# A gate unit moved from the v stage into the scan, a wider parameter tile, and an earlier load of the first initial states

## The chip, the cores and the metric

The kernel runs on one core of a Trainium2 chip. The metric is device microseconds of one execution. A core has TensorE (PE, matmuls; PEld is its weight load), VectorE (DVE), ScalarE (ACT) and GpSimd (POOL), each with its own instruction stream in a fixed order; SyncE (SP) issues the DMAs of this kernel. [...]

## The reference

One step of a hybrid backbone, one layer, with D = 1024, on 1024 latent tokens and 128 context tokens that share the weights:

```python
# sub-layer 1, the token mixers on one normalised and modulated input h
z, xbc, dt_raw, u, v, ga, gb = split(h @ w_in)
x, B, C = split(silu(conv3(xbc)))            # x 2048 wide, B and C 512 wide
y_f, hf = ssd_chunked(x * dt_f, dt_f * A_f, B, C, h0_f)     # chunks of 128, 32 heads of 64
y_b, hb = the same backwards
y_ssd = rmsnorm((y_f + y_b + d * x) * silu(z))
y_sgu = u * (sgu_w @ layernorm(v) + sgu_b)   # per 128-token chunk and 128-channel group
x1 = x0 + gate1 * rmsnorm((sigmoid(ga) * (y_ssd @ w_bs) + sigmoid(gb) * (y_sgu @ w_bu)) @ w_out)
# sub-layer 2, the ConvFFN
up = depthwise3x3(h2 @ w_up);  a, val = split(up)           # 2 x 2816 channels
x2 = x1 + gate2 * rmsnorm((gelu(a) * val) @ w_down)
```

In the chunked scan a state of 128 x 64 per head runs from chunk to chunk; the latent scans start from states given as inputs (h0), the context's scans from zero. Outputs are the tokens and the context's final states.

## The kernel before

All 1152 tokens are kept channel by channel in three blocks of 384 tokens. Every float32 product is made of three matmuls on halves of the operands, high x high, high x low, low x high (`gemm_cm`, L293). The inputs are resident as hh and hl. The weights stream through `Weights` (L58 on): pieces of 128 x 512 (256 KB) are loaded by SP into three raw buffers wr (L70), then split by ACT (a cast into wh, L82) and DVE (a subtraction into wl, L83). There are four buffers of wh and wl; for six of the eight pieces of a v half the room is a pair of larger tiles, vwh and vwl. `W.advance(n)` splits n more pieces and issues the loads that lie three ahead; `W.take(n)` hands out pieces.

A **unit** (`inproj`, L423) makes 128 output channels from two pieces: for each of three token blocks 24 matmuls into a PSUM bank "gps" out of three (`gbank`), an advance by one piece in the second and third block, and a sink that consumes the bank. The **gate unit** (`gate_unit`, L615) has as its sink a copy by ACT into an SBUF tile gt (L618) and a store of gt by SP to a scratch in DRAM (L619), from where the gate is read again much later. Where gt lies and how many buffers it has is set by `gtp`: one buffer in the scan's pool ssdA, three in a pool opened after the scan.

The **scan** works on 16 pairs of heads in 17 rounds. A round interleaves the steps of a pair (transposes ptX, decays R and EP on ACT, yd, yo and state matmuls pst and pstc, H products on DVE) with filler units (x, z, B, C, gate) that keep PE busy. `load_R` and `load_E` bring the decays of a pair from DRAM, `load_H` (L661) its initial states. For the first pair they are issued after the pool ssdA opens, behind the first x unit: R and EP for three segments, then H. The end of a pair (DVE L605, ACT L606 and L608, store L609) multiplies by the gate z and stores to yssd_scr.

After the scan its pools are closed and others opened at the same place. Then comes the **v stage**: for each of two halves of 512 channels, a gate unit, then nine v tiles (`v_tile`): 24 matmuls of 512 columns (L906 to L908) into a bank "pv" from the same three as the gate's, a copy by ACT into vtok (L910), statistics on DVE. The dot products of a modulation run on DVE beside it, and the u units follow.

In the **ConvFFN** the up-projection goes to tiles U; the convolution takes eight of nine taps on DVE (L1200), each acc = U * w + acc with the weight from a parameter tile fpar.

The order within an engine is made by a list scheduler when the program is built: it takes instructions in the order of the code with priorities, so an instruction moved in the code moves others too.

Of the kernel before, what the change touches and what calls it, by code (L numbers as in the profile page):

```python
# [4 lines left out]
F32 = mybir.dt.float32  # L5
# [25 lines left out]
MT_DT, MT_U, MT_B, MT_C, MT_X, MT_Z, MT_GA, MT_GB = 0, 1, 9, 13, 17, 33, 49, 57  # L31
# [75 lines left out]
def body(tc, A, O):  # L107
# [4 lines left out]
    def pool(name, bufs=1, **kw):  # L112
        if kw.get("space") != DRAM:
            kw["reuse_waits"] = "tile"
        cm = tc.tile_pool(name=name, bufs=bufs, **kw)
        return cm, cm.__enter__()

    def close(*cms):
        for cm in cms:
            cm.__exit__(None, None, None)  # L120
# [10 lines left out]
    ga_scr = dr.tile([8, 128, T], F32, name="ga_scr")  # L131
    gb_scr = dr.tile([8, 128, T], F32, name="gb_scr")
# [17 lines left out]
    gate_mts = [MT_GA + i for i in range(8)] + [MT_GB + i for i in range(8)]  # L150
# [46 lines left out]
    W = Weights(nc, wp, plan)  # L197
# [95 lines left out]
    def gemm_cm(ps, parts, kh, kl, cols, first=True, last=True):  # L293

        n = len(parts) * 4
        for k in range(n):
            wh, wl = (p.rearrange("p (k m) -> p k m", m=128)[:, k % 4, :] for p in parts[k // 4])
            xh, xl = kh[:, k, cols], kl[:, k, cols]
            PE.matmul(ps, lhsT=wh, rhs=xh, start=first and k == 0, stop=False)  # L299
            PE.matmul(ps, lhsT=wh, rhs=xl, start=False, stop=False)  # L300
            PE.matmul(ps, lhsT=wl, rhs=xh, start=False, stop=last and k == n - 1)  # L301
# [11 lines left out]
    def gbank(name):  # L313
        return pg.tile([128, 512], F32, tag="g", name=name)
# [71 lines left out]
    parts = {}  # L386
# [33 lines left out]

    def inproj(sink, parts=None):  # L423
        parts = parts or W.take(2)
        for tb in range(NTB):
            ps = gbank("gps")[:, :TB]
            gemm_cm(ps, parts, hh, hl, slice(TB * tb, TB * tb + TB))
            W.advance(1 if tb else 0)
            sink(tb, ps)
            yield  # L430

# [2 lines left out]
    def run_unit(u, step=None):  # L434
        gen, tails = u
        for _ in gen:
            if pending:
                pending.pop(0)()
            if step:
                step()  # L440
        while pending:
            pending.pop(0)()
        pending.extend(tails)
# [119 lines left out]
    def b_unit(g, inp=True):  # L563
        BT = spe.tile([128, GW], F32, tag="BT", name=f"BT{g}")
        Bt = spe.tile([128, NC, 128], F32, tag="Btok", name=f"Btok{g}")
        groups[g] = [BT, Bt]
        return conv_gen(BT, 16 + g, inp), [lambda b=b: to_tok(BT, Bt, f"B{g}", b) for b in range(3)]

    def c_unit(g):
        CT = spb.tile([128, GW], F32, tag="CT", name=f"CT{g}", bufs=2)  # L570

        def cb(b):
            if b == 0:
                groups[g] += [CT, spe.tile([128, 2, NC, 128], F32, tag="CB", name=f"CB{g}")]
            BT, _, _, CB = groups[g]
            pv = tbank(f"pcb{g}{b}")[:, :384].rearrange("p (c i) -> p c i", i=128)
            for i in range(3):
                o = gcol(384 * b + 128 * i)
                PE.matmul(pv[:, i, :], lhsT=BT[:, o:o + 128], rhs=CT[:, o:o + 128], start=True, stop=True)
            for d in range(2):  # L580
                V.tensor_tensor(CB[:, d, 3 * b:3 * b + 3, :], pv, (Lo, Up)[d].unsqueeze(1).to_broadcast([128, 3, 128]), op=ALU.mult)
        return conv_gen(CT, 20 + g), [lambda b=b: cb(b) for b in range(3)]

    def x_unit(q):
        X = spb.tile([128, GW], F32, tag="X", name=f"X{q}", bufs=3)

        def tok(b):
            if b == 0:
                xq[q] = (X, spa.p.tile([128, NC, 128], F32, tag="Xtok", name=f"Xtok{q}", bufs=2))
            to_tok(X, xq[q][1], f"X{q}", b)  # L590
        return conv_gen(X, q), [lambda b=b: tok(b) for b in range(3)]

    def z_unit(q):
        X = xq[q][0]

        def gen():
            zt = spr.tile([128, T], F32, tag="z", name=f"z{q}")

            def sink(tb, ps):
                S.activation(zt[:, TB * tb:TB * tb + TB], ps, AF.Copy, scale=0.5)  # L600
            yield from inproj(sink)
            silu(zt)
            for t0, t1, s in segs(0, T):
                xs = X[:, gcol(t0):gcol(t0) + t1 - t0]
                V.tensor_tensor(xs, xs, zt[:, t0:t1], op=ALU.mult)  # L605
                S.activation(zt[:, t0:t1], xs, AF.Square)  # L606
            V.tensor_tensor(ssq, ssq, zt, op=ALU.add)
            S.activation(X, X, AF.Copy, scale=par[:, P_SN + q:P_SN + q + 1])  # L608
            SP.dma_start(yssd_scr[q], X)  # L609
        return gen(), []  # L610
# [1 line left out]
    class gtp:  # L612
        pass

    def gate_unit(dst, parts=None):  # L615
        def sink(tb, ps):
            o = gtp.p.tile([128, TB], F32, tag="gt", name="gt", bufs=gtp.bufs)
            S.copy(o, ps)  # L618
            SP.dma_start(dst[:, TB * tb:TB * tb + TB], o)  # L619
        return inproj(sink, parts), []  # L620

    def unit_of(mt):
        if mt >= MT_GB:
            return gate_unit(gb_scr[mt - MT_GB])
        if mt >= MT_GA:
            return gate_unit(ga_scr[mt - MT_GA])
        if mt >= MT_Z:
            return z_unit(mt - MT_Z)
        if mt >= MT_X:
            return x_unit(mt - MT_X)  # L630
        if mt >= MT_C:
            return c_unit(mt - MT_C)
        return b_unit(mt - MT_B)
# [18 lines left out]
    def load_E(q, s):  # L652

        cc = cc_of(s)
        E = spa.p.tile([128, 2, 2, 128], F32, tag="EP", name=f"EP{q}{s}", bufs=2)
        for h in range(2):
            SP.dma_start(E[64 * h:64 * h + 64].rearrange("p d c i -> p d (c i)"),
                         acs_scr[q, :, h, cc[0]:cc[0] + 2].rearrange("d c i -> d (c i)").unsqueeze(0).to_broadcast([64, 2, 256]))
        EPt[q, s] = E

    def load_H(q):  # L661
        H = spa.p.tile([128, 8, 2, 128], F32, tag="H", name=f"H{q}", bufs=2)
        SP.dma_start(H[:, 0], A["h0"][q])
        Ht[q] = H
# [157 lines left out]
    def flush():  # L822
        while pending:
            pending.pop(0)()
# [12 lines left out]
    close(u_cm)  # L837
    sa_cm, spa.p = pool("ssdA")
    gtp.p, gtp.bufs = spa.p, 1
    run_unit(first_x)  # L840
    for s in (4, 0, 1):
        load_R(0, s)
        if s < 4:
            load_E(0, s)
    load_H(0)
    after = None
    for q in range(17):
        steps = []
        if q < 16:
            if after is None:  # L850
                flush()
                pro, outs = ssd(q)
                steps += pro + outs
            else:
                steps += after
            after = None
            if q + 1 < 16 and (q + 1) % 4:
                lazy = []

                def nxt_steps(i, q=q, lazy=lazy):  # L860
                    if not lazy:
                        flush()
                        lazy.extend(ssd(q + 1))
                    return lazy[0][i]()
                steps += [lambda i=i, f=nxt_steps: f(i) for i in range(4)]
                after = lazy
        merge(rounds[q], steps)
        if after is not None:
            after = after[1]
    close(sa_cm, sb_cm, se_cm, k_cm, sr_cm)  # L870


# [109 lines left out]
            mod_load1()  # L982

    for h in range(2):
        gate = W.take(2)
        if h == 0:
            v_ahead(8)
        run_unit(gate_unit((gb_scr if gate_mts[h] >= MT_GB else ga_scr)[(gate_mts[h] - MT_GA) % 8], gate))
        if h:
            W.advance(6)  # L990
        parts = W.take(8)
        for c in range(NC):
            cpy = v_tile(h, c, parts)
            if h == 0 and c < 4:
                loads(c)
            if h == 0 and c == 3:
                queue_behind(S.activation(cc, cc, AF.Silu), cpy)
            if h or c >= 4:
                mod_step()
            if h == 0 and c in (6, 7):  # L1000
                bias(c - 6)
            if h and c % 3 == 2:
                layernorm(c // 3)
        W.advance(2)
# [66 lines left out]
    gate = gate_tile(0)  # L1071
# [90 lines left out]


    f_cm, fp = pool("ffn")
    fpar = fp.tile([128, 440], F32, name="fpar")
    SP.dma_start(fpar, A["fpar"])

    U = [[fp.tile([128, 18, 66], F32, name=f"U{i}{j}") for j in range(2)] for i in range(2)]
# [66 lines left out]
    for kk in range(NFF):  # L1235
# [19 lines left out]
        else:  # L1255
            for half in range(1 if kk == 1 else 0, 2):
                parts = W.take(2)
# [138 lines left out]
```

## Time and profile before

| | |
|---|---|
| median of 3 runs | 2447.68 us (2444.17 to 2451.82) |
| the profiled execution | 2446.12 us, span 2444.3 us |
| PE busy | 2396.7 us, 98% of the span |
| DVE / ACT / POOL busy | 1780.6 / 1191.6 / 28.1 us |
| mean granted PE clock | 0.994 |

The profile is one execution. Times of rows are in us from the span's start. A row of a timeline reads: start, duration, engine, line of the kernel, operation, output <- inputs, size, count, and in brackets how long the engine stood idle before it and which instruction ended that. A row of the waits reads: engine and line that waited, what ended the wait, us in total, times, longest. Rows of merged instructions have one start for the group. In a row of windows, the busy time of each engine is followed by the granted clock of PE, the DMA engines' share, and the GB/s. The stages: first weights and modulation to about 50 us, first units to 139, scan 139 to 936, v stage 937 on, ConvFFN taps 1640 to 2240.

### The profile page before, as it was taken

What the parts mean: (1) busy time and instruction counts of PE and PEld (TensorE: products, weight loads), DVE (VectorE), ACT (ScalarE), POOL (GpSimd) and SP (SyncE); (2) the same over time, 40 slices, a digit from 0 to 9 for tenths busy, and PEclk for the clock granted to TensorE, in tenths of its full rate; (3) what the DMA queues carried; (4) which work ended last, traced back from release to release, by engine and by line L of the source; (5) the groups of instructions that cost most, each with busy time, mean ns of one, the idle gap of its engine ahead of it and who ended that gap; (6) DMA issues with size and microseconds to landing.
All of it is one profiled execution on the core that took longest, in us unless ns stands there. A gap on an engine that the chain in (4) does not pass through costs nothing.

```text
span 2444.3 us, 37314 instructions
## 1 busy us (share of the span) xinstructions
PE 2396.7 (98%) x13952; PEld 2267.3 (93%) x13952; DVE 1780.6 (73%) x2754; ACT 1191.6 (49%) x2406; POOL 28.1 (1%) x82
## 2 busy tenths in 40 slices
PE   6989999999999998999999999999999999999998
PEld 4989999999999997899999999999999999998877
DVE  5767787778758764973546657469999989998564
ACT  4586766758647742211435445353333333344443
POOL 0000000000000000000000000000000000000000
PEclk9999999999999999999999999999999999999999
DMA  6144434434424425641556657541222212124674
GB/s 260 35 139 137 120 124 145 136 104 137 140 82 141 152 78 171 214 140 61 162 156 218 198 175 236 155 133 65 69 77 69 72 57 67 61 73 136 216 243 133
DMA packets 204181, 323.20 MB, mean 132 GB/s; under 512 B 19328, under 2 KB 113312, under 8 KB 203872
## 3 DMA queue, kind: packets, MB, share of 16 engines
q1 hardware_dynamic: 204000, 320.82, 41.1%
q8 instruction: 109, 1.79, 0.3%
q14 instruction: 72, 0.59, 0.1%
HBM read 278.22 MB, written 42.52 MB: 131 GB/s over the span
## 4 chain that ended last, share of the span: by engine, by line
PE 90%; DMA 4%; DVE 3%; ACT 1%; issue 1%; SPq 0%; POOL 0%; DVEq 0%; ACTq 0%; POOLq 0%
PE gps L299 11%; PE gps L301 11%; PE gps L300 11%; PE pup L300 7%; PE pup L301 7%; PE pup L299 7%; PE fo L1212 4%; PE fo L1214 4%; PE fo L1213 4%; PE yo L756 2%; PE pbs L301 2%; PE pbs L299 2%; PE pbs L300 2%; PE pv L906 1%; PE pv L907 1%; PE pv L908 1%
## 5 line engine op out<-in xcount | busy, mean ns | idle before, releaser
L83 DVE TENSOR_TENSOR wl<-wr,wh 128x512 fp32r<-128x512 f32 x544 | 372.0, 689 | 270.8 <-ACT wh L82 262.8
L82 ACT CAST wh<-wr 128x512 fp32r<-128x512 f32 x544 | 333.7, 619 | 474.1 <-PE pup L300 121.6
L299 PE MATMUL gps<-hh,wh 128*128 128x384 f32 x1512 | 514.8, 340 | 0.3 <-ACT pad L354 0.3
L301 PE MATMUL gps<-hh,wl 128*128 128x384 f32 x1512 | 513.4, 340 | 0.0
L300 PE MATMUL gps<-hl,wh 128*128 128x384 f32 x1512 | 512.3, 339 | 0.0
L1200 DVE SCALAR_TENSOR_TENSOR acc<-U,fpar,acc 128x960 f32<-128x960 f32 (+1 forms) x352 | 444.2, 1266 | 16.0 <-ACT acc L1193 8.2
L300 PE MATMUL pup<-h2l,wh 128*128 128x384 f32 x1056 | 353.1, 334 | 0.0
L299 PE MATMUL pup<-h2h,wh 128*128 128x384 f32 x1056 | 352.9, 334 | 0.0
L301 PE MATMUL pup<-h2h,wl 128*128 128x384 f32 x1056 | 352.4, 334 | 0.0
L299 PEld LDWEIGHTS gps<-hh,wh 128*128 128x128 f32 x1512 | 284.9, 188 | 2.3 <-issue 1.4
L301 PEld LDWEIGHTS gps<-hh,wl 128*128 128x128 f32 x1512 | 284.7, 188 | 1.7 <-issue 1.7
L300 PEld LDWEIGHTS gps<-hl,wh 128*128 128x128 f32 x1512 | 284.8, 188 | 0.8 <-issue 0.7
L299 PEld LDWEIGHTS pup<-h2h,wh 128*128 128x128 f32 x1056 | 198.2, 188 | 1.4
L300 PEld LDWEIGHTS pup<-h2l,wh 128*128 128x128 f32 x1056 | 198.2, 188 | 1.3
L301 PEld LDWEIGHTS pup<-h2h,wl 128*128 128x128 f32 x1056 | 198.2, 188 | 0.0
L689 ACT ACTIVATE R<-R,nb 128x128 f32<-128x128 f32 x576 | 178.2, 392 | 38.7 <-DMA R<-acs_scr 31.5
L1182 ACT COPY U<-pup 128x384 f32<-128x384 f32 (+1 forms) x132 | 58.4, 442 | 225.2 <-PE pup L301 225.2
L1213 PE MATMUL fo<-wh,gl 128*128 128x512 f32 x384 | 148.3, 396 | 0.0
L1212 PE MATMUL fo<-wh,gh 128*128 128x512 f32 x384 | 148.0, 397 | 0.1
L1214 PE MATMUL fo<-wl,gh 128*128 128x512 f32 x384 | 139.8, 396 | 0.0
L299 PE MATMUL pbs<-ysh,wh 128*128 128x384 f32 x384 | 129.1, 336 | 2.6 <-DVE ga L1110 1.3
L301 PE MATMUL pbs<-ysh,wl 128*128 128x384 f32 x384 | 129.2, 336 | 0.1
(311 smaller groups left out, 3855.5 us busy)
## 6 DMA issues: line engine op xcount, KB each, us to landing
wr<-in_w_dn SPq DMA_DIRECT2D x132, 256.0 KB, 3.0
wr<-in_w_in SPq DMA_DIRECT2D x130, 256.0 KB, 2.8
R<-acs_scr SPq DMA_DIRECT2D x64, 512.0 KB, 4.5
wr<-in_w_bs SPq DMA_DIRECT2D x96, 256.0 KB, 3.4
wr<-in_w_up SPq DMA_DIRECT2D x90, 256.0 KB, 2.6
EP<-acs_scr SPq DMA_DIRECT2D x128, 128.0 KB, 3.2
wmt<-in_w_modt SPq DMA_DIRECT2D x32, 512.0 KB, 3.7
wr<-in_w_bu SPq DMA_DIRECT2D x48, 256.0 KB, 2.9
```

The costliest lines, as they stand in the source:

```text
L82: self.nc.scalar.copy(hi, w)
L83: self.nc.vector.tensor_tensor(lo, w, hi.bitcast(F32), op=ALU.subtract)
L299: PE.matmul(ps, lhsT=wh, rhs=xh, start=first and k == 0, stop=False)
L300: PE.matmul(ps, lhsT=wh, rhs=xl, start=False, stop=False)
L301: PE.matmul(ps, lhsT=wl, rhs=xh, start=False, stop=last and k == n - 1)
L689: S.activation(r, r, AF.Relu, scale=-1.0, bias=nb[:, c, col:col + 1])
L756: PE.matmul(yo[:, d, i, :], lhsT=H[:, k, d, :], rhs=CT[:, 128 * c:128 * c + 128], start=True, stop=True)
L1182: S.copy(u[:, a // 64:b // 64, 1:65], src.rearrange("p (r c) -> p r c", c=64))
L1200: tap = V.scalar_tensor_tensor(av[:, r0:r1], u[:, r0 + dy - 1:r1 + dy - 1, dx:dx + 64], w[i], av[:, r0:r1], op0=ALU.mult, op1=ALU.add)
L1212: PE.matmul(outs[c][h], lhsT=mh[:, cs_], rhs=wh, start=k == 0, stop=False)
L1213: PE.matmul(outs[c][h], lhsT=ml[:, cs_], rhs=wh, start=False, stop=False)
L1214: PE.matmul(outs[c][h], lhsT=mh[:, cs_], rhs=wl, start=False, stop=k == NFF - 1)
```

## The change

Three edits. (1) The first of the two gate units of the v stage now runs at the end of the scan, before its pools close, so its gt tile is the one of the scan's pool, with one buffer; `inproj` takes its two pieces itself and does not advance the weights in this unit. In the v stage, the first half keeps only `v_ahead(8)` (splits of eight pieces at high priority); the second runs a gate unit as usual. (2) The tile fpar has 480 columns, of which the first 440 are used; tiles allocated behind it in the FFN's pool lie 160 bytes further. (3) `load_H(0)` stands right after the pool ssdA opens, ahead of the first x unit and of the loads of R and EP.

```diff
-    def inproj(sink, parts=None):
-        parts = parts or W.take(2)
+    def inproj(sink, ahead=True):
+        parts = W.take(2)
         for tb in range(NTB):
             ps = gbank("gps")[:, :TB]
             gemm_cm(ps, parts, hh, hl, slice(TB * tb, TB * tb + TB))
-            W.advance(1 if tb else 0)
+            if ahead:
+                W.advance(1 if tb else 0)
             sink(tb, ps)
             yield
...
-    def gate_unit(dst, parts=None):
+    def gate_unit(dst, ahead=True):
         def sink(tb, ps):
             o = gtp.p.tile([128, TB], F32, tag="gt", name="gt", bufs=gtp.bufs)
             S.copy(o, ps)
             SP.dma_start(dst[:, TB * tb:TB * tb + TB], o)
-        return inproj(sink, parts), []
+        return inproj(sink, ahead), []
...
     sa_cm, spa.p = pool("ssdA")
     gtp.p, gtp.bufs = spa.p, 1
+    load_H(0)
     run_unit(first_x)
     for s in (4, 0, 1):
         load_R(0, s)
         if s < 4:
             load_E(0, s)
-    load_H(0)
...
+    run_unit(gate_unit(ga_scr[gate_mts[0] - MT_GA] if gate_mts[0] < MT_GB else gb_scr[gate_mts[0] - MT_GB], False))
     close(sa_cm, sb_cm, se_cm, k_cm, sr_cm)
...
     for h in range(2):
-        gate = W.take(2)
         if h == 0:
             v_ahead(8)
-        run_unit(gate_unit((gb_scr if gate_mts[h] >= MT_GB else ga_scr)[(gate_mts[h] - MT_GA) % 8], gate))
-        if h:
+        else:
+            run_unit(unit_of(gate_mts[h]))
             W.advance(6)
...
-    fpar = fp.tile([128, 440], F32, name="fpar")
+
+    fpar = fp.tile([128, 480], F32, name="fpar")[:, :440]
```

**How the order changes.** The names in the rows are the program's tiles with a running number; lines of the changed kernel are up to three higher. First ACT at the end of the scan, from the copy so of the last finished state: before,

```order
L742 COPY so_9260<-pstc_9259 128x256
L82 CAST vwh<-wr_9499 128x512 [waits DMAHW3_49]
L82 CAST vwh<-wr_9503 128x512 [waits DMAHW5_49]
L82 CAST vwh<-wr_9507 128x512 [waits DMAHW6_49]
L760 ACTIVATE EP_9253<-EP_9253 128x512 [waits DMAHW7_49,DMAHW4_49,DVE_49]
...
L606 ACTIVATE z_9372<-X_8645 128x1024 [waits DVE_49]
L608 ACTIVATE X_8645<-X_8645,par 128x1153 [waits Activation_49]
L618 COPY gt<-gps 128x384 [waits PE_49]
L618 COPY gt<-gps 128x384 x2
L910 COPY vtok<-pv_9629 128x512 [waits DMAHW3_49,PE_49,Activation_49]
```

and with the change, where the copies wait for the stores (DMAHW) of the one gt buffer:

```order
L743 COPY so_9260<-pstc_9259 128x256
L619 COPY gt<-gps 128x384 [waits PE_49]
L82 CAST vwh<-wr_9583 128x512 [waits DMAHW3_49]
...
L82 CAST wh_9605<-wr_9595 128x512 [waits DMAHW2_49]
L619 COPY gt<-gps 128x384 [waits DMAHW3_49,PE_49,Activation_49]
L82 CAST wh_9611<-wr_9599 128x512 [waits DMAHW4_49]
...
L619 COPY gt<-gps 128x384 [waits DMAHW1_49,PE_49,Activation_49]
L607 ACTIVATE z_9372<-X_8645 128x128 [waits DVE_49]
L607 ACTIVATE z_9372<-X_8645 128x1024 [waits DVE_49]
L609 ACTIVATE X_8645<-X_8645,par 128x1153 [waits Activation_49]
L913 COPY vtok<-pv_9617 128x512 [waits DMAHW6_49,PE_49,Activation_49]
```

The three gt copies have moved from behind the end of the last pair (L606, L608) to ahead of it, the first ahead of the last three vwh casts.

PE at the same place, before, from the last yd and pstc matmuls of the scan to the first v tile:

```order
L776 MATMUL yd_9349<-RS_9230,Xtok_8858 64x128 [waits DVE_49]
L776 MATMUL yd_9349<-RS_9230,Xtok_8858 64x128 x7
L776 MATMUL pstc_9259<-RSc_8992,Xtok_8858 64x128 [waits Activation_49]
L776 MATMUL pstc_9259<-RSc_8992,Xtok_8858 64x128
L756 MATMUL yo_9340<-CT_7241,H_8823 128x128 [waits DVE_49]
L756 MATMUL yo_9340<-CT_7241,H_8823 128x128 x3
L906 MATMUL pv_9629<-vwh,hh 128x512 [waits Activation_49]
```

and with the change:

```order
L909 MATMUL pv_9617<-vwh,hh 128x512 [waits Activation_49]
L910 MATMUL pv_9617<-vwh,hl 128x512
L911 MATMUL pv_9617<-vwl,hh 128x512
L909 MATMUL pv_9617<-vwh,hh 128x512
L910 MATMUL pv_9617<-vwh,hl 128x512
L777 MATMUL yd_9349<-RS_9230,Xtok_8858 64x128 [waits DVE_49]
L777 MATMUL yd_9349<-RS_9230,Xtok_8858 64x128 x7
L777 MATMUL pstc_9259<-RSc_8992,Xtok_8858 64x128 x2
L911 MATMUL pv_9617<-vwl,hh 128x512
L757 MATMUL yo_9340<-CT_7241,H_8823 128x128 [waits DVE_49]
L757 MATMUL yo_9340<-CT_7241,H_8823 128x128 x3
```

Five matmuls of the first v tile now stand ahead of the scan's last small matmuls.

SP at the first pair, before, behind the stores to acs_scr:

```order
L510 DMA acs_scr<-rows 16x1152 x3
L648 DMA R_1086<-acs_scr 128x4x128 [waits DMAHW6_49,DMAHW1_49,DMAHW7_49,DMAHW0_49,PE_49]
L645 DMA R_1088<-acs_scr 128x4x256 [waits DMAHW3_49,PE_49,Activation_49]
L657 DMA EP_1090<-acs_scr 64x2x256 [waits DMAHW4_49]
L657 DMA EP_1090<-acs_scr 64x2x256 [waits DMAHW5_49]
L645 DMA R_1093<-acs_scr 128x4x256 [waits DVE_49]
L657 DMA EP_1095<-acs_scr 64x2x256 x2
L663 DMA H_1098<-in_h 128x256
L663 DMA H_1405<-in_h 128x256 [waits DMAHW2_49,PE_49]
```

and with the change:

```order
L511 DMA acs_scr<-rows 16x1152 x3
L664 DMA H_970<-in_h 128x256 [waits DVE_49,PE_49]
L649 DMA R_1088<-acs_scr 128x4x128 [waits DMAHW6_49,DMAHW3_49,DMAHW7_49,DMAHW1_49,DMAHW0_49]
L646 DMA R_1090<-acs_scr 128x4x256 [waits DMAHW4_49]
L658 DMA EP_1092<-acs_scr 64x2x256 [waits DMAHW5_49]
L658 DMA EP_1092<-acs_scr 64x2x256
L646 DMA R_1095<-acs_scr 128x4x256
L658 DMA EP_1097<-acs_scr 64x2x256 [waits PE_49]
L658 DMA EP_1097<-acs_scr 64x2x256
L664 DMA H_1405<-in_h 128x256 [waits DMAHW2_49,Activation_49]
```

The first pair's H has moved ahead of the R and EP loads; the second pair's (the last row) has stayed behind them.

## The prediction

> **What bounds the kernel now.** The first view is the page's table of engines, the second PE's waits.
>
> ```profile
> PE 2396.7 (98%) x13952; PEld 2267.3 (93%) x13952; DVE 1780.6 (73%) x2754; ACT 1191.6 (49%) x2406; POOL 28.1 (1%) x82
> ...
> PE pm L223 <- DMA wmod<-in_w_mod: 11.6, 2, 11.3
> PE pv L906 <- ACT gt L618: 8.3, 1, 8.3
> PE yo L756 <- DMA H<-in_h: 4.2, 1, 4.2
> ```
>
> TensorE is busy for 2396.7 of 2444.3 us, so a change that removes no matmul can only work on the 47.6 us in which PE is not busy, or on time in which matmuls run slowly. The three longest waits (total, times, longest) are the first weights, 11.3 us at the kernel's start, which no edit touches; 8.3 us before the v stage; and 4.2 us for H, the first pair's initial state. The last two are the places the diff edits.
>
> The third view cuts the span around these two waits into windows and adds the clock.
>
> ```profile
> core 0: us, PE busy (x) PEld busy (x) DVE busy (x) ACT busy (x) POOL busy (x), PEclk, DMA share, GB/s
> 928.20:931.50 3.30, 0.28 (x3) 0.09 (x1) 3.15 (x8) 1.29 (x3) 0.00 (x0) 1.00 0.61 171
> 931.50:936.80 5.30, 0.03 (x1) 0.04 (x1) 3.72 (x5) 2.76 (x4) 0.00 (x0) 0.50 0.11 38
> 936.80:941.80 5.00, 5.00 (x12) 3.94 (x13) 0.00 (x0) 0.68 (x2) 0.00 (x0) 0.50 0.93 265
> 139.65:143.06 3.41, 0.27 (x3) 0.04 (x1) 0.76 (x2) 3.29 (x10) 0.00 (x0) 1.00 1.11 300
> 146.48:149.89 3.41, 3.41 (x12) 3.33 (x13) 2.06 (x5) 3.41 (x7) 0.00 (x0) 0.50 0.69 209
> ```
>
> After 3.3 us without matmuls the granted clock (PEclk) falls to 0.50, and the first 5 us of work after the wait still run at 0.50. A wait of this length thus costs more than its own row says.
>
> **The transition, the large term.** The timeline of PE, then of ACT, at the end of the scan:
>
> ```profile
> 925.59 1.09 PE L776 MATMUL yd<-RS,Xtok 128*64 128x128 f32 x16
> ...
> 927.32 1.16 PE L756 MATMUL yo<-CT,H 128*128 128x128 f32 x8 [0.42 <-DVE EP L761]
> 936.77 0.79 PE L906 MATMUL pv<-vwh,hh 128*128 128x512 f32 x1 [8.29 <-ACT gt L618]
> ...
> 941.93 0.39 PE L906 MATMUL pv<-vwh,hh 128*128 128x512 f32 x1
> ...
> 944.68 0.39 PE L906 MATMUL pv<-vwh,hh 128*128 128x512 f32 x1
> ...
> 925.32 0.62 ACT L82 CAST wh<-wr 128x512 fp32r<-128x512 f32 x1 [0.35 <-DMA wr<-in_w_v]
> ...
> 931.17 0.31 ACT L606 ACTIVATE z<-X 128x128 f32<-128x128 f32 x1 [1.82 <-DVE X L605]
> ...
> 935.09 1.26 ACT L608 ACTIVATE X<-X,par 128x1153 f32<-128x1153 f32 x1
> 936.25 1.22 ACT L618 COPY gt<-gps 128x384 f32<-128x384 f32 x3
> ```
>
> The three gate banks are full when the last gps matmul ends, but ACT's copies out of them (L618) stand behind the tail of the last pair (L606, L608) and start at 936.25. The first v tile takes the bank of gate block 0, so PE stops. The gate's tile gt had to wait for a room that opens only when the scan's pools close.
>
> The change takes a gt tile in the scan's pool instead, one buffer. The first gt copy then stands on ACT right behind the copy of the finished state, ahead of the later half of the v weights' casts, and the first v tile waits for that alone. In the new order PE issues five pv matmuls after the gate's, then yd, pstc, one pv, yo, and the rest of v. The scan's tail on DVE and ACT (931 to 936) is unaltered and runs beside v matmuls instead of beside an idle PE.
>
> The working, from the start of yd to the first matmul of the second v tile:
> - Now: 944.68 - 925.59 = 19.09 us.
> - The small matmuls yd, pstc and yo are the time from yd to the first pv less the two waits: 936.77 - 925.59 - 8.29 - 0.42 = 2.47 us.
> - A v tile at full clock: rows 941.93 and 944.68 are the 13th and the 25th pv matmul, so 12 take 2.75 us, 0.229 each, and 24 take 5.50 us.
> - After: 2.47 + 5.50 = 7.97 us. The difference is 11.1 us: 8.29 for the wait, 0.42 for yo's wait (pv matmuls now lie ahead of yo) and 2.4 for the 12 half-clock matmuls (941.93 - 936.77 = 5.16 us instead of 2.75).
>
> [...]
>
> What is late next: the weights of the v tile's last pieces are cast by 925.32 + 0.62, with one gt copy (0.41, a third of 1.22) now ahead of the last; PE asks for that piece at about 925.59 + 2.47 + 21 x 0.229 = 932.9, 6 us later. The one gt buffer chains the three copies through their stores: copy 2 waits for store 1 to land, copy 3 for store 2. Behind a waiting copy on ACT stand casts and the tail's L606. The fourth v tile waits for the ACT copy of tile 0, whose destination vtok needs the store of the last X (yssd) landed. Rows for both, SP's first:
>
> ```profile
> 920.99 1.92 SPq L70 DMA_DIRECT2D wr<-in_w_v  x2
> ...
> 925.73 0.33 SPq L70 DMA_DIRECT2D wr<-in_w_in  x1
> ...
> 936.38 0.33 SPq L609 DMA_DIRECT2D yssd_scr<-X  x1
> ...
> yssd_scr<-X SPq DMA_DIRECT2D x16, 576.5 KB, 3.7
> ...
> gb_scr<-gt SPq DMA_DIRECT2D x24, 192.0 KB, 2.9
> ```
>
> A gt store takes 2.9 us. In the new order store 1 goes out behind the first of the two wr loads at 920.99, near 922, and lands near 925, when copy 2 comes; store 2 goes out behind the load of 925.73, near 926.5, and lands near 929.4, before L606 at 931.17 needs ACT. A chain later by 1 us or 2 would still fit. The yssd store lands at 936.38 + 3.7 = 940.1 and the vtok copy (the same size as a cast, 0.6) ends at 940.7. PE wants the fourth tile's bank at 925.59 + 2.47 + 3 x 5.50 = 944.6: slack 3.9 us. So I take the whole 11.1. Bounds of this term: -11.1, and zero if the tail still held PE.
>
> **The first pair, a small term.** PE, then ACT, DVE, SP and H's DMA row:
>
> ```profile
> 139.41 0.52 PE L557 MATMUL ptX<-cst,X 128*128 128x128 f32 x3 [0.36 <-DVE CB L581]
> 144.07 0.79 PE L756 MATMUL yo<-CT,H 128*128 128x128 f32 x2 [4.15 <-DMA H<-in_h]
> 145.03 0.90 PE L557 MATMUL ptX<-cst,X 128*128 128x128 f32 x3 [0.16 <-ACT Xtok L558]
> 146.22 0.80 PE L726 MATMUL pst<-xwf,Btok 128*128 128x128 f32 x2 [0.28 <-DVE xwf L711]
> 146.80 0.69 PE L299 MATMUL gps<-hh,wh 128*128 128x384 f32 x1
> ...
> 142.54 0.61 ACT L706 ACTIVATE EP<-EP 128x512 f32<-128x512 f32 x1
> 143.06 1.55 ACT L689 ACTIVATE R<-R,nb 128x128 f32<-128x128 f32 x5
> 144.52 0.45 ACT L558 COPY Xtok<-ptX 128x384 f32<-128x384 f32 x1
> ...
> 146.29 0.46 ACT L354 COPY pad<-gps 128x384 f32<-128x384 f32 x1
> ...
> 145.00 0.43 DVE L730 TENSOR_TENSOR H<-H,cdk 128x256 f32<-128x256 f32 x1 [0.52 <-DMA H<-in_h]
> ...
> 133.48 0.39 SPq L648 DMA_DIRECT2D R<-acs_scr  x1
> ...
> 138.13 1.45 SPq L663 DMA_DIRECT2D H<-in_h  x2
> ...
> H<-in_h SPq DMA_DIRECT2D x16, 128.0 KB, 4.7
> ```
>
> Now both H loads leave SP at 138.13 to 139.58, behind all R and EP loads. With the change pair 0's load goes ahead of the R loads, before 133.48, while SP waits for the stores that R reads; it delays nothing and lands 4.7 us later, by 138.2. So yo's 4.15 us wait goes. But PE's next needs stand in line. The following ptX group needs the first Xtok copy. On ACT that copy moves ahead of the five R activations; the EP activation still ends only at 143.15, so the copy ends near 143.6 and PE stands from 139.9 till then. The pst matmuls need xwf, which on DVE stands behind pair 1's H product (145.00), whose load stays behind the EP loads, one DMA issue (0.7) earlier: pst at about 145.5 instead of 146.22. Then the x unit's next gps block needs the pad copy, on ACT behind all eight R activations: 143.6 + 8 x 0.31 (1.55 / 5) = 146.1, plus 0.46 = 146.5 against 146.80. The gain is 0.3 us. The long idle stretch stays (139.9 to 143.6), so the half clock up to 149.89 stays too. Bounds: nothing, and everything, 4.15 + 0.16 + 0.28 + 12 matmuls at half speed (3.41 / 2 = 1.7) = 6.3 us. I take 0.3: the ACT rows leave little room.
>
> **Edits at nothing.** The diff's two pieces less of lead: the gate unit at the scan's end no longer advances the weights inside it. The v pieces' casts and loads come out in the same order with the same waits from the v stage on, and the first one stands 6 us ahead as worked out above. The parameter tile: 40 columns more shift every later tile of the FFN by 160 bytes and copy nothing. Would DVE's taps, which read U, fpar and acc, care where their operands lie?
>
> ```profile
> 150.00:700.00 550.00, 548.32 (x3710) 537.30 (x3709) 427.92 (x790) 380.81 (x840) 2.46 (x25) 1.00 0.42 129
> 1650.00:1850.00 200.00, 200.00 (x1118) 195.13 (x1117) 186.43 (x175) 77.28 (x140) 0.00 (x0) 1.00 0.22 71
> ...
> L1200 DVE SCALAR_TENSOR_TENSOR acc<-U,fpar,acc x352: 1208/1219/1421, 1640.6 to 2238.4; 128x960 f32<-128x960 f32 x132, 128x1152 f32<-128x1152 f32 x44
> ```
>
> The taps read U shifted by zero, one or two elements and at several row offsets, and the shorter form shows 1208 at the least and 1219 as the median of all: position does not show. PE is busy for the whole 200 us while DVE is at 93%, so taps dearer by a few per cent would still hide. Cost 0, with a bound in the rivals. In the scan's rounds 0 to 11 the scheduler reorders some small groups; PE loses 550 - 548.3 = 1.7 us there, so a gain is at most 1.7, a loss open; I take 0.
>
> **Sum.** -11.1 - 0.3 = -11.4 us. The profiled execution took 2446.12 us (span 2444.3, 1.8 around it), so its like would take 2434.7. It lies 1.6 below the median of the runs, 2447.68; the median goes to 2436.3. I predict 2436.
>
> **Rivals.**
> 1. *Something behind the gate takes over part of the wait.* The single gt buffer or vtok's room stops ACT or the fourth v bank. For: a chain of two store landings and a shared ACT queue, with the weights loading at the same time. Against: 3.9 us of slack. Should the yssd store land at 8 us rather than 3.7, PE would stand for 0.4; to give back 3 us the tail itself must be 7 us later. Time: -11.4 + 3 = -8.4, 2439; up to 2442.
> 2. *The first pair's wait goes entirely.* If Xtok's copy gets onto ACT early enough that PE's idle stretch breaks, up to 6.3 us instead of 0.3: -17.4, 2430. Against: the EP activation till 143.15 stands ahead of it on ACT.
> 3. *The change does not do what it says at the transition.* The v tile waits for the scan's tail by another way (its weights' room, a closed pool), and the 8.29 reappear under another name: only 0.3 to 1 remain, 2447. Against: the first pv waits for the ACT copy alone in the new order, and its last weights were cast by 925.9 before too.
> 4. *Slower: DVE's taps.* If the moved tiles make L1200 dearer, DVE becomes the FFN's bound. The taps run from 1640.6 to 2238.4, 598 us, with 7% or 41 us of air; 352 at the median 1219 ns are 429 us, so DVE binds from 41 / 429 = 9.5% on, and the gain is used up at 52 / 429 = 12%. At 15% the loss is 64 - 41 = 23 us; 2436 + 23 = 2459. For: DVE is the fullest engine beside PE there. Against: the narrow spread of L1200. The reordered scan rounds are the same sign: over 1 us in each of the 11 rounds would eat the gain, and PE's 1.7 us lost in 550 speaks against it.
>
> **Chances.** Forecast 0.72, rival 1 0.11, rival 2 0.07, rival 3 0.05, rival 4 0.05. The likeliest case by itself spans 2432 to 2440: the three runs of before lie 7.7 us apart, so a median can be off by 2 or 3, and the bounds of the small terms are +-1. To leave out no more than 2 in 10, the range reaches to most of rivals 1 and 2: 2430 to 2443. About 0.3%, 7.3 us, is what a measurement of this kernel can tell from no change: below 2440.3 counts as faster. That is the forecast, rival 2 and part of rival 1, less what noise takes: 0.82. Within: 0.14; slower: 0.04.
>
> **What would show it.** In the changed profile: no PE wait at L909 (pv) above 1 us, granted clock 1.00 over 925 to 945, yo's wait at the last pair gone; the rows of the tail (L607, L609) beside pv matmuls; v tiles 5.5 us apart from the first on; the sum of PE's idle time near 38 instead of 47.6. At the first pair, no wait of yo for H, but 3 to 4 us of ptX on ACT Xtok in its stead, and the x unit's block at 146.5. L1200's median still 1219. Wrong if pv or a vtok copy shows a wait of several us near 940, if ACT's gt copies 2 and 3 start after 931, or if PE shows new waits between 150 and 700.

## The result and the profile after

The changed kernel takes 2429.55 us (median of 6 runs, 2426.64 to 2435.24), the kernel before 2448.85 us (median of 6, 2444.17 to 2451.82): a ratio of 0.9926, 95% interval 0.9909 to 0.9943. That is 18 us less (14 to 22), where 11.4 had been forecast; the median lies half a microsecond below the lower end of the stated range. The profiled execution took 2428.39 us with a span of 2426.6, 17.7 less than before, and the accounts below are made on that.

The page's table of engines and PE's waits, after:

```profile
PE 2387.9 (98%) x13952; PEld 2266.8 (93%) x13952; DVE 1779.4 (73%) x2754; ACT 1191.0 (49%) x2406; POOL 27.8 (1%) x82
...
PE pm L223 <- DMA wmod<-in_w_mod: 10.7, 2, 10.4
PE ptX L558 <- ACT Xtok L559: 2.2, 1, 2.2
...
PE pst L727 <- DVE xwf L712: 1.5, 1, 1.5
...
PE fo L1215 <- ACT wh L82: 1.1, 3, 0.6
```

Both waits that the prediction started from are gone from the list: pv on the ACT copy of gt, and yo on H. In their place stand 2.2 and 1.5 us at the first pair; the wait of fo, 1.1 us, is new too and comes up below. But look at the busy time. PE is not busy for 2426.6 - 2387.9 = 38.7 us instead of 47.6, which accounts for 8.9 of the 17.7. The other 8.8 are *busy* time that has become shorter, with the same 13952 matmuls. A shorter half-clock stretch was forecast to bring 2.4 of it. The rest was not in the forecast.

The transition, PE's timeline, then ACT's, then the same three windows as before:

```profile
924.15 0.34 PE L301 MATMUL gps<-hh,wl 128*128 128x384 f32 x1
924.33 0.39 PE L909 MATMUL pv<-vwh,hh 128*128 128x512 f32 x1
...
925.57 1.09 PE L777 MATMUL yd<-RS,Xtok 128*64 128x128 f32 x16
...
927.15 1.05 PE L757 MATMUL yo<-CT,H 128*128 128x128 f32 x8
...
932.16 0.39 PE L909 MATMUL pv<-vwh,hh 128*128 128x512 f32 x1
...
915.71 0.48 ACT L619 COPY gt<-gps 128x384 f32<-128x384 f32 x1
...
928.90 0.48 ACT L619 COPY gt<-gps 128x384 f32<-128x384 f32 x1
930.68 0.31 ACT L607 ACTIVATE z<-X 128x128 f32<-128x128 f32 x1 [1.30 <-DVE X L606]
...
940.50 1.07 ACT L913 COPY vtok<-pv 128x512 f32<-128x512 f32 x2 [3.90 <-DMA yssd_scr<-X]
...
928.20:931.50 3.30, 3.30 (x17) 2.68 (x16) 2.40 (x6) 1.31 (x3) 0.00 (x0) 1.00 0.74 236
931.50:936.80 5.30, 5.30 (x25) 4.40 (x24) 3.96 (x5) 2.32 (x2) 0.00 (x0) 1.00 0.06 24
936.80:941.80 5.00, 5.00 (x24) 4.14 (x23) 0.69 (x2) 1.07 (x2) 0.00 (x0) 1.00 0.90 257
```

PE goes from the gate's last matmul into the v tile without a break, the granted clock stays at 1.00, and the second v tile starts at 932.16 instead of 944.68. From the last gps matmul to there it takes 932.16 - 924.15 = 8.01 us instead of 944.68 - 925.33 = 19.35: 11.3 us less. The rest of the 17.7 is found by comparing the starts of the same instructions. Rows of before, then of after:

```profile
129.40 2.46 SPq L510 DMA_DIRECT2D acs_scr<-rows  x4
...
925.33 0.33 PE L301 MATMUL gps<-hh,wl 128*128 128x384 f32 x1
...
146.80:149.84 3.04, 3.04 (x10) 3.04 (x10) 2.01 (x5) 3.04 (x5) 0.00 (x0) 0.50 0.76 231
```

```profile
127.64 2.47 SPq L511 DMA_DIRECT2D acs_scr<-rows  x4
...
143.41 0.69 PE L299 MATMUL gps<-hh,wh 128*128 128x384 f32 x1
...
L1203 DVE SCALAR_TENSOR_TENSOR acc<-U,fpar,acc x352: 1206/1219/1421, 1628.2 to 2224.7; 128x960 f32<-128x960 f32 x132, 128x1152 f32<-128x1152 f32 x44
...
143.41:148.69 5.28, 5.28 (x18) 5.28 (x17) 3.73 (x8) 5.28 (x12) 0.00 (x0) 0.50 0.39 137
```

It is 1.8 before the first pair (the stores to acs_scr start at 127.64 instead of 129.40, ahead of anything that was changed), 1.6 at the first pair (to the x unit's gps block, 143.41 instead of 146.80), 2.2 lost again in the scan, 11.3 at the transition, and 5.3 behind the first FFN tap, which starts at 1628.2 instead of 1640.6. Half of what the scan loses is clock: behind the first pair the gps matmuls ran at 0.50 for 5.28 us instead of 3.04, which costs half the difference, 1.1 us. That is not the early load's doing: by the starts of the gps matmuls this stretch lasts 3.0, 5.5 and 5.3 us in the profiles of before and of the first two experiments, which load late, and 5.3, 4.3 and 3.3 in those of the change and of the third and fourth, which load early. Where the other half of the 2.2 went is not found; PE's idle time in the scan is 1.7 us in both.

The last term is the surprise. The first fence has two rows of the groups of instructions and a window in the middle of the down projection before, the second the same after:

```profile
L1213 PE MATMUL fo<-wh,gl 128*128 128x512 f32 x384 | 148.3, 396 | 0.0
...
L906 PE MATMUL pv<-wh,hh 128*128 128x512 f32 x36 | 14.0, 389 | 0.0
...
2280.00:2330.00 50.00, 50.00 (x215) 40.17 (x215) 23.32 (x38) 20.27 (x38) 0.00 (x0) 1.00 0.57 180
```

```profile
L1216 PE MATMUL fo<-wh,gl 128*128 128x512 f32 x384 | 146.2, 390 | 0.0
...
L909 PE MATMUL pv<-wh,hh 128*128 128x512 f32 x36 | 14.0, 389 | 0.0
...
2280.00:2330.00 50.00, 50.00 (x223) 41.39 (x222) 24.58 (x43) 22.56 (x43) 0.54 (x1) 1.00 0.57 185
```

In both kernels PE is busy for the whole of these 50 us at clock 1.00 and waits for nothing, yet after the change it starts 223 matmuls in them instead of 215. The matmuls fo of the down projection have become as fast as pv, which has the same shape and operand types: 390 ns each instead of 396, and from start to start, the mean of consecutive fo without the longest twentieth, 227.2 ns instead of 233.8. With 1188 of them this is up to 7.8 us. From the first to the last fo it is 755.6 us instead of 760.9, only 5.3 less, because the faster stream now runs into the casts of its own weights: the new wait of fo for ACT's wh. Eight intervals between consecutive fo are longer than 260 ns, 4.2 us in sum, where the kernel before had two, 0.8 us; at 0.23 us each without a wait, that gives back 2.0 us.

### The profile page after: what moved, and what is told of

Same layout as the page of the kernel before. It is cut to its first block, busy times and chain, and to the rows that moved or that the text cites. A ratio compares the mean times of both kernels' runs of the same rounds, so it can differ in the third digit from the quotient of the medians.

```text
span 2426.6 us, 37310 instructions
## 1 busy us (share of the span) xinstructions
PE 2387.9 (98%) x13952; PEld 2266.8 (93%) x13952; DVE 1779.4 (73%) x2754; ACT 1191.0 (49%) x2406; POOL 27.8 (1%) x82
## 4 chain that ended last, share of the span: by engine, by line
PE 79%; DMA 3%; DVE 2%; ACT 1%; issue 1%; SPq 0%; DVEq 0%; POOLq 0%; ACTq 0%
PE gps L300 8%; PE gps L301 8%; PE gps L299 8%; PE pup L300 8%; PE pup L301 8%; PE pup L299 8%; PE fo L1215 3%; PE fo L1216 3%; PE fo L1217 3%; PE pbs L299 2%; PE pbs L301 2%; PE pbs L300 2%; PE yo L757 2%; PE pv L911 1%; PE pv L909 1%; PE pv L910 1%
```

## The experiments

Two theories stood against each other. **The forecast's**: the gate edit brings all there is, the parameter tile nothing. **The rival from the trace**: the gate edit brings 11, and moving the FFN's tiles by 160 bytes speeds up the down projection. Four kernels take the change apart.

### One: the gate edit alone

The edit against the kernel before, without the new arguments of `inproj` and `gate_unit`, which are as in the whole change:

```diff
+    run_unit(gate_unit(ga_scr[gate_mts[0] - MT_GA] if gate_mts[0] < MT_GB else gb_scr[gate_mts[0] - MT_GB], False))
     close(sa_cm, sb_cm, se_cm, k_cm, sr_cm)
...
     for h in range(2):
-        gate = W.take(2)
         if h == 0:
             v_ahead(8)
-        run_unit(gate_unit((gb_scr if gate_mts[h] >= MT_GB else ga_scr)[(gate_mts[h] - MT_GA) % 8], gate))
-        if h:
+        else:
+            run_unit(unit_of(gate_mts[h]))
             W.advance(6)
```

> The gate edit alone, with the parameter tile and the first load as before. Forecast as it stood: -11.1 us, ratio 0.9955, PE's wait before the v tiles gone and the clock at 1.00 there. Rival (the gate edit brings the whole 18 us seen, through a better order afterwards): -17 or more, 0.993. Down projection matmuls (fo) 0.234 us from start to start in both.

Measured: ratio 0.9951 (0.9939 to 0.9964), that is 12.0 us less (9 to 15). The windows of its profile over the transition and the down projection:

```profile
2280.00:2330.00 50.00, 50.00 (x215) 40.20 (x214) 22.48 (x37) 20.80 (x38) 0.00 (x0) 1.00 0.53 172
925.00:945.00 20.00, 20.00 (x107) 16.39 (x106) 10.49 (x18) 7.09 (x11) 0.00 (x0) 1.00 0.64 202
```

PE is busy through the whole transition at full clock, and the down projection is as slow as before (215). The transition term is right by mechanism and, within the interval, by size, and it is not the whole result.

### Two: the wider parameter tile alone

```diff
-    fpar = fp.tile([128, 440], F32, name="fpar")
+    fpar = fp.tile([128, 480], F32, name="fpar")[:, :440]
```

> The wider parameter tile alone. Forecast as it stood: 0 us, ratio 1.000. Rival (the shift of the FFN's tiles by 160 bytes speeds up the matmuls of the down projection): fo matmuls 0.227 us from start to start instead of 0.234, the whole kernel 5 to 7 us shorter, ratio 0.9975; DVE's taps unchanged at 1219 ns.

Measured: ratio 0.9976 (0.9967 to 0.9985), 5.9 us less (4 to 8). One line that declares 40 unused columns makes the kernel faster. The window and the taps' row:

```profile
2280.00:2330.00 50.00, 50.00 (x222) 41.40 (x222) 23.25 (x38) 20.93 (x38) 0.00 (x0) 1.00 0.57 184
...
L1200 DVE SCALAR_TENSOR_TENSOR acc<-U,fpar,acc x352: 1204/1219/1422, 1637.6 to 2234.1; 128x960 f32<-128x960 f32 x132, 128x1152 f32<-128x1152 f32 x44
```

The fo matmuls come every 227.1 ns, and the taps' median is 1219 ns as before. The gain is on PE, not on DVE, and the forecast's zero for this edit is refuted.

### Three: the earlier load alone

```diff
     gtp.p, gtp.bufs = spa.p, 1
+    load_H(0)
     run_unit(first_x)
...
-    load_H(0)
```

> The earlier load of the first initial states alone. Forecast as it stood: -0.3 us, a wait for Xtok and xwf in place of the one for H. Rival from the trace of the changed kernel: -1.6 us at the first pair, taken back by new stalls of 2 us in the scan near 380 us, in sum 0; ratio 0.9993 to 1.0003, not to be told from 1 by the total, so it is read from the trace.

Measured: ratio 1.0005 (0.9996 to 1.0015): no change that can be told, between 1 us less and 4 more. The first pair did become shorter, which its trace shows. From the first store to acs_scr to the x unit's next gps matmul it is 144.89 - 128.75 = 16.1 us, against 146.80 - 129.40 = 17.4 in the kernel before. In the three profiles without the early load this takes 17.4, 18.0 and 18.1 us, in the eleven with it (the change and the runs below among them) 15.6 to 17.0, with a mean of 16.1. The rows of this run:

```profile
128.75 2.47 SPq L510 DMA_DIRECT2D acs_scr<-rows  x4
...
142.18 0.68 PE L557 MATMUL ptX<-cst,X 128*128 128x128 f32 x3 [2.84 <-ACT Xtok L558]
143.27 0.79 PE L726 MATMUL pst<-xwf,Btok 128*128 128x128 f32 x2 [0.41 <-DVE xwf L711]
144.89 0.69 PE L299 MATMUL gps<-hh,wh 128*128 128x384 f32 x1 [0.82 <-ACT pad L354]
```

The wait for H has split into the three waits that the forecast named, on Xtok, xwf and pad. The rival's new stalls are not there: from 144.89 to the scan's last gps matmul at 923.76 PE is idle for 0.9 us, before for 1.7. Up to there this profile is 1.6 us ahead (923.76 against 925.33); it loses that only behind the scan (the first tap starts at 1641.7, before at 1640.6), and why is not shown.

### Four: the change without the wider tile

The edit against the changed kernel:

```diff
-    fpar = fp.tile([128, 480], F32, name="fpar")[:, :440]
+    fpar = fp.tile([128, 440], F32, name="fpar")
```

> The changed kernel with the parameter tile back at 440 columns. Forecast as it stood: all of the change, so the same time as the changed kernel, ratio to before 0.9926. Rival (the parameter tile carries 5 to 6 us): 0.995, and fo matmuls back at 0.234 us from start to start.

Measured: ratio 0.9950 (0.9937 to 0.9962). The gate and the load together are the gate alone (0.9951). With the tile's 0.9976, a product of 0.9926, they make the whole. The fo matmuls go with the tile in all four experiments: 233.8 ns in the three with 440 columns, 227.1 in the one with 480.

### What is it about the place?

In the program as built, the operands of fo lie as follows, in bytes along a partition: the moving wh and wl start at 32 bytes past a multiple of 256, their buffers 2048 bytes apart; the stationary gh and gl are 1536 bytes apart, with column blocks of 512 bytes. So the distance from any wh or wl to any gh or gl leaves one remainder by 256, whichever buffers meet. It is 96 with 440 columns and 0 with 480. For pv (stationary hh, moving wh or vwh) it is 0 in both kernels. Four more kernels move the tiles: the widths 448, 456 and 464, of which the first is shown, and one, with 480 columns, that has everything from the weights' buffers on shifted by 32 bytes, which leaves fo's distance at 0 and makes pv's 224 (the second part):

```diff
-    fpar = fp.tile([128, 480], F32, name="fpar")[:, :440]
+    fpar = fp.tile([128, 448], F32, name="fpar")[:, :440]
...
+    wp.tile([128, 8], F32, name="wpad")
     W = Weights(nc, wp, plan)
```

> The changed kernel with 448 columns: the FFN's later tiles lie 32 bytes further than with 440 instead of 160. The split gate tiles gh, gl then start at 32 bytes past a multiple of 64 and of 128, 160 past one of 256; the weights wh, wl start at 32 past a multiple of 256. If the distance of the two matters by 64 or 128 bytes: fo 0.227 us from start to start. If by 256, or if it was the size of the move: 0.234.

> 456 columns: gh, gl 64 bytes further than with 440, again at a multiple of 64. If the rest by 64 bytes decides: fo back at 0.234 us, although the tiles have moved; by the theory that any move away from 440's places helps: 0.227.

> 464 columns: gh, gl 96 bytes further, 32 past a multiple of 64, 96 past one of 128, while the weights are at 32. If the rest by 64 decides: fo 0.227 us; if the rest by 128: 0.234.

> The changed kernel with an unused tile of 32 bytes ahead of the weights' buffers, so that the weights wh, wl and everything behind them, gh and gl too, start at a multiple of 64; hh and hl stay at 32 past one. If it is the two operands' places relative to each other that matter: fo stays at 0.227 us (both at 0), and the v tiles (pv, stationary hh at 32, moving wh at 0) go from 0.227 to 0.234. If it is the place of the stationary operand alone: fo 0.234 and pv 0.227. If the rest of the stationary weights matters for the 384-column matmuls as well, gps and pup rise above 0.173 us.

And two further ones, 488 and 496 columns, for the remainders still missing:

> 488 columns: gh, gl lie at a distance from the weights of 32 bytes past a multiple of 256 (480 columns: 0). If the distance's rest by 256 decides, with odd multiples of 32 the slow ones: fo 0.233 to 0.234 us. If what counts is only to be far enough from 440's place: 0.227.

> 496 columns: a distance of 64 past a multiple of 256. If even multiples of 32 other than 0 are in between, as 128 and 192 were: 0.228 to 0.232 us. If 64 is as good as 0: 0.227; if it is as bad as the odd ones: 0.234.

Measured, as the mean from start to start of consecutive fo (or pv) matmuls without the longest twentieth:

| kernel | from moving to stationary operand, mod 256 | ns |
|---|---|---|
| 480 columns (the change), fo | 0 | 227.2 |
| shifted weights, fo | 0 | 226.7 |
| the change, pv | 0 | 226.8 |
| 488, fo | 32 | 233.0 |
| 496, fo | 64 | 233.0 |
| 440 (before), fo | 96 | 233.8 |
| 448, fo | 128 | 231.6 |
| 456, fo | 160 | 233.0 |
| 464, fo | 192 | 228.9 |
| shifted weights, pv | 224 | 233.2 |

The kernel with shifted weights decides between the two operands' places relative to each other and the stationary tile's own place. Its pv rows among the groups of instructions, then the same in the changed kernel:

```profile
L910 PE MATMUL pv<-wh,hh 128*128 128x512 f32 x36 | 14.2, 396 | 0.0
L912 PE MATMUL pv<-wl,hh 128*128 128x512 f32 x36 | 14.2, 395 | 0.0
```

```profile
L909 PE MATMUL pv<-wh,hh 128*128 128x512 f32 x36 | 14.0, 389 | 0.0
L911 PE MATMUL pv<-wl,hh 128*128 128x512 f32 x36 | 14.0, 389 | 0.0
```

Here hh has not moved at all, and pv has gone from 389 to 396 ns because the weights moved against it; fo, whose stationary tiles now lie at a multiple of 64 as in the slow kernel before, is fast. So it is the distance that counts, and not the place of the stationary tile.

The finer expectations fared worse. A remainder by 64 or by 128 fails as a rule: 448 and 464 should have been alike and fast by the first, and 464 slow by the second. That even multiples of 32 lie in between holds for 128 and 192, not for 64. What the table bears out is only that a distance of a multiple of 256 bytes was the fastest in all three instances, and every other tried one slower, by 2 to 7 ns.

The end of the down projection tests this once more inside each kernel. For 36 of the last fo matmuls the moving operand is not in wh but in a tile wacc of the FFN's own pool. It moves together with gh and gl, and as built its distance from them leaves 0 in every kernel, whatever the width. Rows of the kernel before, where the distance from wh leaves 96:

```profile
2428.53 0.40 PE L1213 MATMUL fo<-wh,gl 128*128 128x512 f32 x1
...
2430.87 0.40 PE L1214 MATMUL fo<-wl,gh 128*128 128x512 f32 x1
...
2431.34 0.39 PE L1213 MATMUL fo<-wacc,gl 128*128 128x512 f32 x1
...
2433.60 0.39 PE L1214 MATMUL fo<-wacc,gh 128*128 128x512 f32 x1
2433.83 0.40 PE L1212 MATMUL fo<-wh,gh 128*128 128x512 f32 x1
...
2436.40 0.40 PE L1214 MATMUL fo<-wl,gh 128*128 128x512 f32 x1
...
2423.93 0.69 DVE L83 TENSOR_TENSOR wl<-wr,wh 128x512 fp32r<-128x512 f32 x1 [0.74 <-ACT wh L82]
```

From wh and wl ten intervals take 2.34 us, 234 ns each; from wacc ten take 2.26, 226 each; from wh again eleven take 2.57, 234 each. Nothing writes to the weights' buffers by then: the last subtraction into wl, the last row, ends at 2424.62. So the slow pace does not need those writes, and a clash with them is not its cause. The runs of wacc also show that the fast pace needs a start: in every kernel whose wh is at another distance the last twelve in a row end at 226 to 227 ns, but up to ten intervals of 224 to 236 can come first, and where single wacc matmuls alternate with wh the pace is not reached. The first v tile of the change, at distance 0, has the same start: 224 to 236 ns up to 929.7 (the restart behind yo apart), 226 to 227 from then on. What is settled in these stretches is not shown.

For the 384-column matmuls the pace showed no such effect: pup is at 173.3 ns and gps at 174 with the shifted weights, where their two operands are 32 apart by the same measure, as in the change, where it is 0; only the mean time of one is longer, 337 ns against 334 and 342 against 340. Why 512 columns differ is not shown.

The totals of a single run each (448: 2432.75 us, 456: 2433.33, 464: 2431.26, shifted weights 2433.53, 488: 2433.87, 496: 2433.34, with the kernel before at 2446.33 beside the first four and 2444.04 beside the others) are all above the 2429.55 of the change, but single runs differ by as much.

### Two checks of the forecast's steps

Both pairs' states loaded first, which takes away H from the wait of xwf:

```diff
+        if q in Ht:
+            return
...
     load_H(0)
+    load_H(1)
```

> The changed kernel with the second pair's initial states also loaded first. If pair 1's H product, ahead of xwf on DVE, is what held the pst matmuls for 1.5 us: that wait ends with Xtok instead, near 141.1 (pst 1.5 us sooner), and the x unit's next block is then held by ACT's pad copy, so that the first pair ends no more than 0.4 us sooner. If H is not what holds it: pst stays where it is. Total 0 to -0.5 us.

```profile
139.24 0.52 PE L558 MATMUL ptX<-cst,X 128*128 128x128 f32 x3 [0.18 <-DVE CB L582]
142.45 0.55 PE L558 MATMUL ptX<-cst,X 128*128 128x128 f32 x3 [2.70 <-ACT Xtok L559]
142.91 0.61 PE L729 MATMUL pst<-xwf,Btok 128*128 128x128 f32 x2
145.16 0.69 PE L299 MATMUL gps<-hh,wh 128*128 128x384 f32 x1 [1.64 <-ACT pad L354]
```

The pst matmuls no longer wait: 142.91 is 3.7 us behind the ptX of 139.24, where the changed kernel has 4.8 (137.93 to 142.75). H was what held xwf. But gps now waits 1.64 us for ACT's pad copy, and from that ptX to gps it is 5.9 us against 5.5: nothing is won. ACT's row of activations sets the end of the first pair here, as the forecast had it. Total 2427.71 us in a single run.

Two gt buffers in the scan's pool:

```diff
-    gtp.p, gtp.bufs = spa.p, 1
+    gtp.p, gtp.bufs = spa.p, 2
```

> The changed kernel with two buffers of gt in the scan's pool instead of one. By the forecast the chain of copies through one buffer was hidden: second v tile still 7.8 to 8.0 us behind yd, total 0. By the first rival the chain costs something: the last pair's tail (L607) or a v tile starts sooner and the total falls by 0.5 to 3 us.

```profile
926.09 0.39 PE L909 MATMUL pv<-vwh,hh 128*128 128x512 f32 x1
...
929.49 1.16 PE L757 MATMUL yo<-CT,H 128*128 128x128 f32 x8 [0.41 <-DVE EP L762]
...
934.62 0.39 PE L909 MATMUL pv<-vwh,hh 128*128 128x512 f32 x1
```

From the first pv matmul (926.09) to the second v tile (934.62) it takes 8.5 us, against 924.33 to 932.16, 7.8, in the change, and yo waits 0.41 us again; the tail's L607 starts 6.6 us behind the first pv, against 6.35. Nothing starts sooner with the second buffer: no sign that the one buffer cost anything. (The expectation measured from yd; since yd now lies behind five pv matmuls, the first pv is the fair start.) Total 2429.99 us in a single run.

## Why the prediction was right and where it was wrong

*The transition: right.* 11.1 us were forecast, 11.3 measured in the trace and 12.0 (9 to 15) by the gate edit alone. Each part held: the wait gone, yo's wait gone, the clock at 1.00, with no idle stretch left. What was to be late next was not late either. The tail's L607 found ACT free at 930.68, and the first vtok copy, held by the yssd store as forecast, ran at 940.50 against a forecast of 940.1; PE did not stop at the fourth tile. That the 2.4 us of half clock would go with the wait was the author's estimate from the windows of before, 0.50 in the second and the third; the three windows of the change, all at 1.00, bear it out. Why the clock fell before is not shown.

*The first pair: right in what takes over, too small by about 1.4 us.* Forecast -0.3. Between the acs_scr stores and the x unit's gps block the profiles with the early load are shorter by 1.7 us (means of 17.9 and 16.1). The step that was mis-sized is the one that let the EP activation end at the same time as before: the first R activation on ACT stands 7.5 to 8.1 us behind the stores with the early load and 8.4 to 8.7 without it, so the whole chain on ACT started about 1 us earlier. H ahead of the R loads did not only delay nothing; R landed sooner. Why is not shown. The second EP activation, which stood ahead of the pad copy before, moved behind it; the forecast's sum has no term for it there and so came out right on this point. By the total the load alone is nothing (1.0005, at best 1 us less), so what the pair wins does not reach the end. In the changed kernel's trace the scan behind it is 2.2 us longer, 1.1 of it by a longer half clock; the forecast kept the half clock but gave it no price beside its 0.3.

*The parameter tile: wrong.* The failed step is "Cost 0". It asked whether an engine's instructions care where their operands lie, and asked it of DVE alone, where the answer was no (1219 ns before and after). But gh and gl, allocated behind fpar in the same pool, are PE's stationary operand, and PE is the bound: 6.6 ns in the mean on the matmuls of the down projection, and 5.9 us (4 to 8) by the experiment. The rival on the slower side, taps made dearer by their place, had the right kind of cause on the wrong engine and with the wrong sign. The profile of before had the hint: two groups of the same shape and type, fo and pv, at 396 and 389 ns.

*Reordered scan rounds and the shorter lead of the weights: right at nothing,* as far as PE's idle time tells: it is busy for 548.26 of 550 us between 150 and 700, before 548.32.

The forecast's sum of 11.4 was thus short by the parameter tile. The first rival (waits behind the gate) and the third (no effect at the transition) are out; the second (all of the first pair's wait gone) gave nearly the time that was measured, 2430, for a reason that did not occur.

## What to carry to other kernels

A wait on the engine that sets the end can cost more than its row: here 8.3 us had 2.4 of half clock behind them, and both went when the blocked copy was taken out from behind an unrelated tail: look for what stands ahead of the releasing instruction on its own engine. An edit that only moves addresses is not free by default (here 160 bytes were worth 5.9 us): ask it of every engine that reads the moved tiles, the bound one first. When two groups of one shape differ by a few ns in the means of the profile, multiply by the count before calling it nothing.

## What the hardware showed that was not expected

With PE busy without a gap at clock 1.00, 128x512 matmuls came every 226.7 to 227.2 ns when the moving and the stationary operand lay a multiple of 256 bytes apart, and every 228.9 to 233.8 ns at the other distances tried (32 to 224 in steps of 32). Inside one trace, that of the kernel before, the pace changed with the place of the moving tile, from 234 ns to 226 and back to 234, after the last write to the weights' buffers. In the runs the two operands' distance changed the interval by up to 3%, 226.7 against 233.8 ns, while neither address alone did: seven places of wacc and gh by 256, always 0 apart, all came to 226 to 227 ns. Why the distance counts is not shown.
